# Tracing each group's heads of a state-space mixer ahead of the next group's input products

## The chip, the cores and the metric

The kernel runs on one core of one Trainium2 chip. The metric is the device time of one execution in microseconds (us); lower is better. The engines are named as in the profile: PE (TensorE matmul), PEld (its weight loads), DVE (VectorE), ACT (ScalarE), POOL and SP (which issues the DMAs).

## The reference, cut to what matters

The reference runs a block of two layers and then a second block of two layers on 256 tokens of width 1024. The first block's first layer is an attention mixer and a feed-forward part. Its second layer is the state-space mixer that the change is in (`mamba2_mixer`), followed by a mixture of experts. The second block has two more layers and is not touched.

```python
def mamba2_mixer(h, w_in, conv_w, conv_b, dt_bias, a_log, d_skip, norm_g, w_out):
    proj = h @ w_in
    z = proj[..., :D_INNER]
    xbc = jax.nn.silu(causal_depthwise_conv(proj[..., D_INNER:D_INNER + CONV_DIM], conv_w, conv_b))
    ...
    y = ssd_chunked(xs, dt, a, bm, cm) + d_skip.astype(jnp.float32)[:, None] * xs
    yg = (y * jax.nn.silu(z)).reshape(bsz, seq, SSM_GROUPS, D_INNER // SSM_GROUPS)
    yf = yf * lax.rsqrt(jnp.mean(yf * yf, axis=-1, keepdims=True) + EPS)
    y = (yf.reshape(bsz, seq, D_INNER) * norm_g.astype(jnp.float32)).astype(h.dtype)
    return y @ w_out
```

There are 32 heads of 64 columns in 4 groups of 8. A group thus has 512 columns of `xs` (convolved) and 512 of the gate `z`. A norm is taken over each group by itself, and the output product sums over all four groups (16 slices of 128 rows of `w_out`).

## The kernel before, in words

Activations lie transposed: 128 features on the partitions, 256 tokens along the row. A product takes its weights as float32, loads them by SP in pieces of 1 MB (`load`, tile `raw`, 5 buffers), and splits each piece into two parts of 1024 elements a row: a rounded part `whi` (ACT, L156, 5 buffers) and the rest `wlo` (DVE, L159, 4 buffers). Each 128 x 128 slice of weights then takes three matmuls (`mm3`, L183 to L185). A product of 256 columns over 1024 rows is 48 matmuls into one PSUM bank: `acc` (2 banks) or `s` (3 banks).

The mixer `mamba` first makes `bc` and `dt`, then for each group g four input products in the order conv, z, conv, z. A `conv` product is scaled by ACT (L936), summed over its shifted copies by DVE (L939, three instructions for each 128 columns) and passed through Silu by ACT (L940). A z product is only passed through Silu into `zz[g]` (L1021). For the last group, z is not made there: it is traced behind the heads of group 0, copied (L1080) and passed through Silu later (L1082).

`tokens(g)` transposes a group's `xs` and scales it by `dt` into `xd` (L1032 on PE, L1033 on DVE). `heads(g)` does for each head three small bf16 matmuls into an `s` bank `pe` (L1044 to L1046, here called a triple), three Exp on ACT into `de` (L1049, 2 buffers) and a product with `cb` on DVE into `m` (L1051, 4 buffers). Two heads are then multiplied with `xd` side by side into half of the one `po` bank (L320, eight matmuls, here called a pair), and DVE adds the result into `xs` (L1058). `norm(g)` multiplies `xs` by `zz` (L1061), squares (L256), folds and sums (L239, L241, L249), takes the root (L231, L274 to L278), spreads it (L286, L287) and writes the group's output rows as two parts (L301, L303, L304). These go into slots of a pool of 12 that also holds `xs`, `zz` and the mixer's input `h`.

The output product is 256 columns at a time: `outs[n]` is a generator over the 16 slices of `w_out`, and `next(o)` traces one slice of weights with six matmuls. In the kernel before, the sums for n = 0 and 1 begin in the two `acc` banks at group 0's norm, the one for n = 2 in an `s` bank at the end, and n = 3 after these. `flush` and `route_shift` finish the leftover sums of the modulation vectors (L503, L505) and a router shift (L1107, L1109).

The context is opened with `schedule_with_timeline_sim=True` (L1714). The order in which the instructions are traced is their precedence; a planner makes from it one fixed order for each engine ahead of the run. Where nothing traced earlier is ready by the planner's own times, an instruction that is traced later takes the place. Each engine then works its list strictly in that order.

Of the kernel before, what the change touches and what calls it, by code (L numbers as in the profile page):

```python
# [13 lines left out]
AF = mybir.ActivationFunctionType  # L14
# [6 lines left out]
KT = 8  # L21
# [61 lines left out]
class K:  # L83
# [833 lines left out]
    def mamba(self):  # L917
        nc, i = self.nc, self.i
        v = nc.vector
        w = i["ssm_w_in"][0]  # L920
        self.nslot = 12
        with ExitStack() as c:
            p = c.enter_context(self.tc.tile_pool(name="ssm", bufs=1))
            h = self.xnorm(self.hilo_s(p, KT), self.gs[1][:, 0], self.mod(1, 0), 0)
# [4 lines left out]
            def conv(n0, out):  # L929

                a = self.gemm(w, KT, D * 2 + n0, 256, h, s=n0 == 2560)
                k0 = n0 // P
                for j in range(2):
                    k = k0 + j
                    o = out[:, j]
                    nc.scalar.activation(o, a[:, j], AF.Identity, bias=cb[:, k : k + 1], scale=cw[:, 72 + k : 73 + k])  # L936
                    for s in (1, 2, 3):
                        wc = cw[:, (3 - s) * 24 + k : (3 - s) * 24 + k + 1]
                        v.scalar_tensor_tensor(o[:, s:], a[:, j, : T - s], wc, o[:, s:], ALU.mult, ALU.add)  # L939
                nc.scalar.activation(out, out, AF.Silu)  # L940
# [70 lines left out]
                nc.scalar.copy(t, pc)  # L1011
                cbt.append(t)
            xs, zz = [], []
            for g in range(4):
                xs.append(self.slot(p))
                zz.append(self.slot(p))
                for j in range(2):
                    s2 = slice(2 * j, 2 * j + 2)
                    conv(g * 512 + j * 256, xs[g][:, s2])
                    if g < 3:  # L1020
                        nc.scalar.activation(zz[g][:, s2], self.gemm(w, KT, g * 512 + j * 256, 256, h), AF.Silu)  # L1021
            y = ([], [])
            wo = i["ssm_w_out"][0]
            acc, outs = [], []

            def tokens(g):

                xd = p.tile([P, 2, 8, 64], F32, tag="xd", bufs=2, name=self.name("xd"))
                for t in range(2):
                    px = self.sm([P, 4, P])  # L1030
                    for j in range(4):
                        nc.tensor.transpose(px[:, j], xs[g][:, j, t * P : (t + 1) * P], self.ident)  # L1032
                    v.tensor_mul(xd[:, t], px.rearrange("p j (b e) -> p (j b) e", e=64),  # L1033
                                 dt[:, t, g * 8 : g * 8 + 8].unsqueeze(2).broadcast_to([P, 8, 64]))
                return xd

            def heads(g, xd):
                for j in range(4):
                    if j % 2 == 0:
                        py = self.po()  # L1040
                    for b in range(2):
                        hd = g * 8 + 2 * j + b
                        pe = self.s([P, 3, P])
                        mm(pe, sel[:, hd : hd + 1].broadcast_to([96, P]), r3, start=True, stop=False, skip_group_check=True)  # L1044
                        mm(pe[:, 0], idb, msl, start=False, stop=True, skip_group_check=True)
                        mm(pe[:, 2], idb, msl, start=False, stop=True, skip_group_check=True)  # L1046
                        de = p.tile([P, 3, P], F32, tag="de", bufs=2, name=self.name("de"))
                        for q3 in range(3):
                            nc.scalar.activation(de[:, q3], pe[:, q3], AF.Exp, bias=rb[:, q3, hd : hd + 1])  # L1049
                        m = p.tile([P, 3 * P], F32, tag="m", bufs=4, name=self.name("m"))  # L1050
                        v.tensor_mul(m, de.rearrange("p a b -> p (a b)"), cbt[g])  # L1051
                        o = py[b * 64 : b * 64 + 64, j % 2]
                        if b == 0:
                            av = []
                        av.append([(o, xd[:, 0, 2 * j + b], m[:, :T], True, False), (o[:, P:], xd[:, 1, 2 * j + b], m[:, T:], False, True)])
                    self.side_by_side(*av)
                    o = xs[g][:, j]
                    v.scalar_tensor_tensor(o, o, self.dcol[:, g * 4 + j : g * 4 + j + 1], py[:, j % 2], ALU.mult, ALU.add)  # L1058

            def norm(g):  # L1060
                v.tensor_mul(xs[g], xs[g], zz[g])  # L1061
                t = [self.slot(p, F32R) for _ in range(2)]
                yl = [[s[:, k] for k in range(4)] for s in t]
                for b in range(2):
                    y[b].extend(yl[b])
                self.norm([xs[g][:, j] for j in range(4)], 512, self.cols["ssm_norm"][:, g * 4 : g * 4 + 4], *yl,
                          src=[xs[g][:, j : j + 2] for j in (0, 2)])

            xd = tokens(0)
            for g in range(5):  # L1070
                if g == 1:
                    self.flush()
                    self.route_shift()
                nxt = tokens(g + 1) if g < 3 else None
                if g < 4:
                    heads(g, xd)
                xd = nxt
                if g == 0:
                    for j in range(2):
                        nc.scalar.copy(zz[3][:, 2 * j : 2 * j + 2], self.gemm(w, KT, 1536 + j * 256, 256, h))  # L1080
                if g == 3:
                    nc.scalar.activation(zz[3], zz[3], AF.Silu)  # L1082
                if g:
                    if g == 1:
                        acc = [self.acc() for _ in range(2)]
                        outs = [self.gemm_steps(wo, 16, n * 256, 256, y, acc[n]) for n in range(2)]
                    norm(g - 1)
                    if g == 4:

                        acc.append(self.s())  # L1090
                        outs.append(self.gemm_steps(wo, 16, 512, 256, y, acc[2]))
                        for k in range(12):
                            next(outs[2])
                    for o in outs:
                        for k in range(4):
                            next(o)
            self.hf = self.raw().rearrange("p (k t) -> p k t", k=KT)
            for n in range(4):
                self.resid(acc[n] if n < 3 else self.gemm(wo, 16, 768, 256, y), n * 256, self.mod(1, 2))
# [618 lines left out]
```

## Time and profile before

| | us |
|---|---|
| median of 3 runs | 2644.95 (2644.51 to 2650.42) |
| the profiled execution | 2647.27 |
| its span, first to last instruction | 2645.5 |
| PE busy in the span | 2573.8 (97%) |
| DVE busy | 1972.3 (75%) |
| ACT busy | 1560.9 (59%) |

The span is what lies between the first and the last instruction of the profiled execution. Busy time of PE is pipelined time: an instruction's row is longer than its distance to the next one. A granted clock of 1.00 is 2.4 GHz, and half of it 1.2 GHz. The mixer's loop over groups lies at about 430 to 625 us of the span.

### The profile page before, as it was taken

To read this page: it belongs to the slowest core of one execution; us is meant where nothing else is said; L and a number is where in the kernel's file an instruction comes from. 1 tells how busy PE (TensorE), PEld (TensorE's weight loads), DVE (VectorE), ACT (ScalarE), POOL (GpSimd) and SP (SyncE) were. 2 spreads that over 40 slices of the span, in tenths; PEclk is the share of its full clock that TensorE was granted. 3 is DMA by queue.
4 is the path that set the end of the run, shared out by engine and by line. 5 is a ranking of instruction groups with operands and counts; after the bars stand their busy time and mean duration, and the time that the engine had idled before them with its cause. 6 is when DMAs were issued, how large, how long until landed. Compare 5 with 4: busy or idle time off the path is not lost.

```text
span 2645.5 us, 46204 instructions
## 1 busy us (share of the span) xinstructions
PE 2573.8 (97%) x18463; PEld 2358.8 (89%) x18463; DVE 1972.3 (75%) x3010; ACT 1560.9 (59%) x2189; POOL 6.4 (0%) x27
## 2 busy tenths in 40 slices
PE   8989998989999998999999999999999999999998
PEld 5779998978888887888878999989999999989998
DVE  5776668786999997989888765677665656677664
ACT  4444436674878876777777444675444444675443
POOL 0000000000000000000000000000000000000000
PEclk8989999998999999999999999999999999999999
DMA  9768767416999997999997556525556557525552
GB/s 309 241 230 273 263 188 228 157 60 227 351 363 348 359 372 277 349 363 341 343 368 265 159 176 213 161 69 167 185 175 199 179 180 219 159 65 176 177 182 88
DMA packets 450829, 608.60 MB, mean 230 GB/s; under 512 B 21563, under 2 KB 308816, under 8 KB 450608
## 3 DMA queue, kind: packets, MB, share of 16 engines
q1 hardware_dynamic: 450246, 605.26, 68.4%
q8 instruction: 146, 2.39, 0.4%
q0 software_dynamic: 176, 0.26, 0.1%
q14 instruction: 75, 0.61, 0.1%
q10 hardware_dynamic: 186, 0.07, 0.0%
HBM read 604.50 MB, written 1.05 MB: 229 GB/s over the span
## 4 chain that ended last, share of the span: by engine, by line
PE 59%; DVE 1%; issue 0%; ACT 0%; DVEq 0%; ACTq 0%
PE acc L184 10%; PE acc L183 10%; PE acc L185 10%; PE s L185 3%; PE s L184 3%; PE s L183 3%; PE acc L1283 3%; PE acc L1282 3%; PE acc L1284 3%; PE acc L1306 1%; PE acc L1305 1%; PE acc L1307 1%; PE s L320 1%; PE po L320 1%; PE sm L910 1%; DVE wlo L159 1%
## 5 line engine op out<-in xcount | busy, mean ns | idle before, releaser
L156 ACT CAST whi<-raw 128x1024 fp32r<-128x1024 f32 x816 | 838.6, 1038 | 714.1 <-PE acc L184 431.4
L159 DVE TENSOR_TENSOR wlo<-raw,whi 128x1024 fp32r<-128x1024 f32 x816 | 972.6, 1204 | 292.1 <-PE acc L185 206.0
L183 PE MATMUL acc<-hl,whi 128*128 128x256 f32 x2336 | 668.1, 286 | 6.1 <-DVE s L643 4.6
L184 PE MATMUL acc<-hl,whi 128*128 128x256 f32 x2336 | 663.5, 284 | 1.1 <-DVE hl L308 0.8
L185 PE MATMUL acc<-hl,wlo 128*128 128x256 f32 x2336 | 662.4, 284 | 0.0
L183 PEld LDWEIGHTS acc<-hl,whi 128*128 128x128 f32 x2336 | 443.9, 190 | 9.2 <-DVE s L643 4.8
L184 PEld LDWEIGHTS acc<-hl,whi 128*128 128x128 f32 x2336 | 443.4, 190 | 4.0 <-issue 1.5
L185 PEld LDWEIGHTS acc<-hl,wlo 128*128 128x128 f32 x2336 | 443.4, 190 | 0.6
L159 DVE TENSOR_TENSOR wlo<-more,whi 128x1024 fp32r<-128x1024 f32 x237 | 281.7, 1220 | 20.1 <-PE acc L1283 6.8
L1283 PE MATMUL acc<-wlo,xh 128*128 128x512 f32 (+1 forms) x768 | 288.4, 376 | 0.8
L1282 PE MATMUL acc<-whi,xh 128*128 128x512 f32 (+1 forms) x768 | 288.9, 378 | 0.0
L1284 PE MATMUL acc<-whi,xl 128*128 128x512 f32 (+1 forms) x768 | 285.9, 373 | 0.0
L156 ACT CAST whi<-more 128x1024 fp32r<-128x1024 f32 x237 | 243.1, 1049 | 42.7 <-PE acc L1284 27.0
L184 PE MATMUL s<-hl,whi 128*128 128x256 f32 x880 | 249.1, 283 | 0.0
L185 PE MATMUL s<-hl,wlo 128*128 128x256 f32 x880 | 249.1, 283 | 0.0
L183 PE MATMUL s<-hl,whi 128*128 128x256 f32 x880 | 248.6, 283 | 0.0
L1283 PEld LDWEIGHTS acc<-wlo,xh 128*128 128x128 f32 x768 | 144.4, 188 | 27.9 <-DVE wlo L159 4.4
L1282 PEld LDWEIGHTS acc<-whi,xh 128*128 128x128 f32 x768 | 144.3, 188 | 25.8
L183 PEld LDWEIGHTS s<-hl,whi 128*128 128x128 f32 x880 | 166.8, 190 | 0.0
L1284 PEld LDWEIGHTS acc<-whi,xl 128*128 128x128 f32 x768 | 144.3, 188 | 25.2
L185 PEld LDWEIGHTS s<-hl,wlo 128*128 128x128 f32 x880 | 166.6, 189 | 0.0
L184 PEld LDWEIGHTS s<-hl,whi 128*128 128x128 f32 x880 | 166.5, 189 | 0.0
(477 smaller groups left out, 4065.3 us busy)
## 6 DMA issues: line engine op xcount, KB each, us to landing
raw<-in_moe_w_gate_dram SPq DMA_DIRECT2D x50, 1024.0 KB, 7.3
raw<-in_moe_w_up_dram SPq DMA_DIRECT2D x48, 1024.0 KB, 7.3
raw<-in_ffn_wg_dram SPq DMA_DIRECT2D x44, 1024.0 KB, 5.3
raw<-in_ffn_wu_dram SPq DMA_DIRECT2D x44, 1024.0 KB, 5.3
raw<-in_moe_w_down_dram SPq DMA_DIRECT2D x43, 1024.0 KB, 6.9
more<-in_moe_w_up_dram SPq DMA_DIRECT2D x40, 1024.0 KB, 7.4
more<-in_moe_w_gate_dram SPq DMA_DIRECT2D x38, 1024.0 KB, 6.8
raw<-in_w_in_dram SPq DMA_DIRECT2D x38, 1024.0 KB, 5.4
```

Source lines behind the costliest of these rows:

```text
L156: i = nc.scalar.copy(hi, src[:, k0 : k0 + m])
L159: nc.vector.tensor_sub(lo, src[:, k0 : k0 + m], hi)
L183: mm(out, whi, xhi, start=first, stop=False, skip_group_check=True)
L184: mm(out, whi, xlo, start=False, stop=False, skip_group_check=True)
L185: mm(out, wlo, xhi, start=False, stop=last, skip_group_check=True)
L320: m = self.nc.tensor.matmul(o, w, x, start=start, stop=stop, skip_group_check=True)
L910: nc.tensor.transpose(ptp[:, b * P : (b + 1) * P], pe[:, b * P : (b + 1) * P], self.ident)
L1282: mm(a, xh[:, k], hi, start=k == 0, stop=False, skip_group_check=True)
L1283: mm(a, xh[:, k], lo, start=False, stop=False, skip_group_check=True)
L1284: mm(a, xl[:, k], hi, start=False, stop=k == 7, skip_group_check=True)
L1305: mm(a, fh[k], hi, start=k == 0, stop=False, skip_group_check=True)
L1306: mm(a, fh[k], lo, start=False, stop=False, skip_group_check=True)
```

## The change

The input products of a group become a function `group(g)`, and z of the last group is made like the others (Silu straight from PSUM; the copy and the late Silu are gone). The trace order becomes: group 0; then for g = 0, 1, 2 the heads of g followed by the input products of g + 1; then the tokens of group 3, `flush`, `route_shift`, the norm of group 0, the heads of group 3. Only behind all of these are the three sums of the output opened (n = 0 and 1 in `acc`, n = 2 in an `s` bank), and every step then traces four slices in all three. The norm of group 1 is traced ahead of the first step, the norms of groups 2 and 3 ahead of the second.

```diff
-            for g in range(4):
+            def group(g):
                 ...
                     conv(g * 512 + j * 256, xs[g][:, s2])
-                    if g < 3:
-                        nc.scalar.activation(zz[g][:, s2], self.gemm(w, KT, g * 512 + j * 256, 256, h), AF.Silu)
+                    nc.scalar.activation(zz[g][:, s2], self.gemm(w, KT, g * 512 + j * 256, 256, h), AF.Silu)
...
-            xd = tokens(0)
-            for g in range(5):
+            group(0)
+            for g in range(3):
+                heads(g, tokens(g))
+                group(g + 1)
+            xd = tokens(3)
+            self.flush()
+            self.route_shift()
+            norm(0)
+            heads(3, xd)
+            acc = [self.acc() for _ in range(2)] + [self.s()]
+            outs = [self.gemm_steps(wo, 16, n * 256, 256, y, acc[n]) for n in range(3)]
+            for g in range(4):
+                if g < 2:
+                    norm(g + 1)
                 if g == 1:
-                    self.flush()
-                    self.route_shift()
-                nxt = tokens(g + 1) if g < 3 else None
-                if g < 4:
-                    heads(g, xd)
-                xd = nxt
-                if g == 0:
-                    for j in range(2):
-                        nc.scalar.copy(zz[3][:, 2 * j : 2 * j + 2], self.gemm(w, KT, 1536 + j * 256, 256, h))
-                if g == 3:
-                    nc.scalar.activation(zz[3], zz[3], AF.Silu)
-                if g:
-                    if g == 1:
-                        acc = [self.acc() for _ in range(2)]
-                        outs = [self.gemm_steps(wo, 16, n * 256, 256, y, acc[n]) for n in range(2)]
-                    norm(g - 1)
-                    if g == 4:
-
-                        acc.append(self.s())
-                        outs.append(self.gemm_steps(wo, 16, 512, 256, y, acc[2]))
-                        for k in range(12):
-                            next(outs[2])
-                    for o in outs:
-                        for k in range(4):
-                            next(o)
+                    norm(3)
+                for o in outs:
+                    for k in range(4):
+                        next(o)
```

## Rows read from the trace of the kernel before

**Rows 1.** The page's first part: busy time, share of the span, instructions.

```profile
PE 2573.8 (97%) x18463; PEld 2358.8 (89%) x18463; DVE 1972.3 (75%) x3010; ACT 1560.9 (59%) x2189; POOL 6.4 (0%) x27
```

**Rows 2.** Stretches: length, busy PE, PEld, DVE, ACT, POOL; PE clock, DMA share, GB/s.

```profile
430.00:542.10 112.10, 110.43 (x925) 106.62 (x924) 82.09 (x124) 80.77 (x123) 0.00 (x0) 0.98 0.53 170
542.10:609.00 66.90, 58.50 (x469) 50.48 (x468) 53.96 (x138) 40.61 (x97) 0.00 (x0) 0.95 0.19 64
...
440.00:460.00 20.00, 18.33 (x158) 17.39 (x158) 17.06 (x25) 17.70 (x31) 0.00 (x0) 1.00 0.68 228
...
563.00:575.00 12.00, 8.29 (x73) 5.12 (x69) 11.85 (x38) 9.15 (x32) 0.00 (x0) 1.00 0.27 87
```

**Rows 3.** Groups of PE instructions from 542.1 to 609 us.

```profile
L183 PE MATMUL acc<-g,whi 128*128 128x256 f32 x65 | 18.5, 295 | 1.4 <-ACT g L303 1.4
L183 PE MATMUL s<-g,whi 128*128 128x256 f32 x32 | 9.1, 285 | 0.5 <-ACT whi L156 0.5
L320 PE MATMUL po<-m,xd 128*64 128x256 f32 x44 | 7.6, 427 | 2.0 <-DVE m L1051 1.3 <-DVE g L1058 0.7
L1044 PE MATMUL s<-r,sel 96*128 96x384 bf16 x18 | 5.7, 332 | 1.4 <-ACT de L1049 1.1
L287 PE MATMUL sm<-dg,ones 128*128 128x128 f32 x16 | 3.5, 325 | 2.8 <-DVE dg L286 2.7
L1032 PE MATMUL sm<-cst,g 128*128 128x128 f32 x8 | 1.7, 345 | 0.0
L249 PE MATMUL sm<-ones,sq 128*128 128x1 f32 x12 | 1.6, 234 | 0.0
```

**Rows 4.** PE in order of time: the pace of undisturbed matmuls, first and last of 47.

```profile
592.37 0.28 PE L183 MATMUL s<-g,whi 128*128 128x256 f32 x1
...
597.82 0.28 PE L184 MATMUL s<-g,whi 128*128 128x256 f32 x1
```

**Rows 5.** PE in order of time, around the end of the input products and after.

```profile
542.33 0.87 PE L320 MATMUL po<-m,xd 128*64 128x256 f32 x8
543.13 0.34 PE L1044 MATMUL s<-r,sel 96*128 96x384 bf16 x1
...
543.42 0.33 PE L1044 MATMUL s<-r,sel 96*128 96x384 bf16 x1
...
546.80 0.69 PE L287 MATMUL sm<-dg,ones 128*128 128x128 f32 x2 [2.67 <-DVE dg L286]
...
584.16 0.54 PE L183 MATMUL acc<-g,whi 128*128 128x256 f32 x2 [0.99 <-ACT g L303]
...
585.51 0.41 PE L183 MATMUL acc<-g,whi 128*128 128x256 f32 x1
```

**Rows 6.** Groups of DVE instructions from 542.1 to 609 us.

```profile
L1051 DVE TENSOR_TENSOR m<-de,cb 128x384 f32<-128x384 f32 x19 | 10.4, 552 | 3.4 <-ACT de L1049 3.1
L1058 DVE SCALAR_TENSOR_TENSOR g<-g,dcol,po 128x256 f32<-128x256 f32 x11 | 5.2, 473 | 0.0
L606 DVE SCALAR_TENSOR_TENSOR xT<-acc,mod,xT 128x256 f32<-128x256 f32 x4 | 1.8, 480 | 6.1 <-PE acc L185 6.1
L159 DVE TENSOR_TENSOR wlo<-raw,whi 128x1024 fp32r<-128x1024 f32 x10 | 12.1, 1222 | 3.1 <-PE acc L185 2.5 <-PE s L185 0.6
```

**Rows 7.** PE and then ACT in order of time, heads between two z products.

```profile
457.46 0.22 PE L1046 MATMUL s<-msl,idb 128*128 128x128 bf16 x1
459.33 0.39 PE L183 MATMUL acc<-g,whi 128*128 128x256 f32 x1 [1.65 <-ACT g L1021]
...
453.73 1.66 ACT L1049 ACTIVATE de<-s,rb 128x128 f32<-128x128 f32 x6
455.24 2.13 ACT L156 CAST whi<-raw 128x1024 fp32r<-128x1024 f32 x2
457.38 1.28 ACT L1021 ACT_TABLE_LOAD   x1
458.68 0.60 ACT L1021 ACTIVATE g<-acc 128x512 f32<-128x512 f32 x1
```

## The prediction, as it was put on record

> **What bounds the kernel now.** I read the page's first part, then the busy time by stretch of the mixer, then PE in order of time there, and last the groups of DVE and ACT instructions. PE is busy for 97% of the span [rows 1], so time can only come from places where PE waits, and the stretches show them. From 430 to 542.1 us, while input products are left, PE is busy 110.43 of 112.1 us. From 542.1, the end of the last z product, to 609.0, the end of the three interleaved output sums, it is busy 58.50 of 66.9 us, with the granted clock at 0.95 on the mean [rows 2]. I call them the input stretch and the tail. From 609 to 625 us the fourth output product runs alone and I expect nothing of it to change.
>
> Busy PE is not PE at its peak, so I price the tail's work. Forty-seven undisturbed matmuls span 5.45 us, 0.1185 us each [rows 4]. The tail has 97 slices of three [rows 3]: 291 x 0.1185 = 34.5 us. It has eleven pairs (44 of the wide L320 form, four to a pair) at 0.80 us, the distance to the next instruction [rows 3, 5]: 8.8 us. Its 18 triples [rows 3] lie 0.29 us apart [rows 5]: 5.2 us. The 36 transposes, sums and spreads [rows 3], taken at the plain pace of 0.12 us, are 4.3 us. Together 52.8 us, so 14.1 of the 66.9 us are lost. The largest single loss is at 543.9 us, where PE waits 2.67 us for the norm's spread. Matmuls after the wait at 584 us are 0.21 us apart instead of 0.12: that is 1.2 GHz in place of 2.4 [rows 5]. In the middle of the tail DVE is the one that is full: 11.85 of 12 us from 563 to 575, with PE at 8.29 [rows 2]. So the tail is held by the elementwise work of 18 late heads and of the norms, for which there are too few products to run beside.
>
> **The change part by part.**
>
> *Work moved out of the tail.* Behind the last z product only the four pairs of group 3 need be left, and I take six triples (two heads done ahead; `m` has room for four, so four to eight). Seven pairs (5.6 us), twelve triples (3.5) and the four transposes of the last tokens (0.5) go: 9.6 us of PE work moves into the input stretch. That stretch has 1.67 us of idle PE, so all 9.6 us lengthen it. No matmul is saved.
>
> *The tail that is left.* PE: 52.8 - 9.6 = 43.2 us. DVE: 53.96 us [rows 2] less twelve `m` at 0.55 (6.6), seven L1058 at 0.47 (3.3), and the 1.8 us of L606 that follow the sums [rows 6]: 42.3 us. ACT had 40.61 us [rows 2] and loses twelve heads of Exp (36 at 0.28 us, by six in 1.66 [rows 7]) and the copy and Silu of the last z, so it does not govern. PE and DVE are nearly even, therefore neither hides the other's start and end. I add 5 us: the wait for the first output rows (here 1.4 us by L303 [rows 3]), the wait at the last norm (0.99 in the row, some 2 with the gaps beside it) and one stretch at the lower clock [rows 5]. The bounds are 0 (everything beside products) and 14.1 (as lost before). Tail after: 48.2 us, 18.7 less.
>
> *Three output sums instead of two from the first step.* This is what gives PE products while the norms of groups 1 to 3 and heads 3 run: 72 matmuls (8.5 us) a step instead of 48. Each stream holds the second half of its split weights until the next group's rows are there. With four `wlo` buffers and three streams one buffer is free, and a split takes some 2.3 us (DVE 1.22 in [rows 6], ACT some 1.05 in [rows 7]) against 2.8 us for the 24 matmuls of a chunk. It fits without a margin; if DVE is late, up to six splits of 2.3 us would show (13.8), if not, nothing. I put it inside the 5 us. The third `s` bank is asked for behind the last heads, so these have three banks first. The same eight loads of 1 MB go through SP, in another order, with the DMA engines 19% busy in the tail [rows 2]; at nothing.
>
> *Heads ahead of the next input products.* Now their instructions go first wherever they are ready, on PE, ACT and DVE. What waits behind them is the next group's splits, convolution and Silu, and through the two `acc` banks PE. By totals there is room: PE 112.1 + 9.6 us, DVE 82.09 + 9.9, ACT 80.77 and 10 for twelve heads of Exp at 0.28 each [rows 2, 7]. The order is the question. One such place exists: at 457.5 us, with the heads of group 0 just run, PE waits for a z product to leave its bank, because ACT does casts, loads the table for Silu (1.28 us) and only then empties it; the distance is 1.87 us, 1.8 of it lost [rows 7]. I take one such stall for each of the three head groups inside the input stretch: 5.4 us, against 1.67 us there before: +3.7. The bounds: none at all (-1.7), and one for each of the four Silus a group, twelve in all (21.6, +19.9).
>
> *The last z with the others, `flush` and `route_shift` ahead of norm 0.* The copy of the last z and its late Silu were ACT work with a table load on either side; its removal is in the tail's numbers. The one-column sums and the router shift are the same matmuls in another place, at nothing; the low clock behind them (some 1.7 us) may come elsewhere, so -1.7 to +1.7.
>
> **Sum:** -18.7 (tail) + 9.6 (work moved) + 3.7 (stalls) = -5.4 us. The profiled execution took 2647.27 us, its span 2645.5 and 1.77 us lie around it; with the change 2641.9. The median before is 2.32 us below that execution, so for a median I expect 2644.95 - 5.4 = 2639.5.
>
> What the Trainium skill would make of it stands by itself. The page "ScalarE: Activation LUTs", section "Rules for kernel authors", says to group functions by table set and finish one set before switching, and its section "What ACT_TABLE_LOAD costs" gives about 2.66 us a switch with the drain. The change mixes Exp with Silu, so the rule speaks against it. This case's rows show 1.28 us for the load and the next instruction right behind it [rows 7]. By the page's price each stall would be 1.4 us dearer and the sum about -1.2 us.
>
> **The rivals.**
>
> *B, no new stall.* The planner finds places for the heads, and DVE and PE overlap all but 2 us of the tail: -21.7 + 9.6 = -12.1, 2632.9. For it: in the input stretch PE waits only 1.67 us although 14 heads already run there, and from 460 us on there is no wait to speak of. Against: those heads filled gaps; now they come first.
>
> *C, the tail stays held by DVE.* The four norms and the last heads are a chain through DVE, and DVE was full where PE waited. Group 3 has its own heads, then its norm, and the norms of groups 2 and 3 both come ahead of the second step. If 10 us of the 14.1 remain lost, the tail is 53.2 (-13.7) and the sum -13.7 + 9.6 + 3.7 = -0.4: 2644.5. The planner doing by itself most of what the new order asks for ends here too, as the first heads already run among the products of group 1.
>
> *D, slower: ACT's tables stop PE in the input stretch.* Each group has four Silus. If Exp of the heads lies between each two of them, ACT switches eight times a group (10.2 us by the load's 1.28), each bank is emptied late, and each time PE loses 1.8 us as at 457.5 [rows 7]: -18.7 + 9.6 + 19.9 = +10.8, 2655.8. It turns the result from six stalls on (6 x 1.8 - 1.67 = 9.1, the rest of the sum). For it: where heads came close together, from 440 to 460 us, ACT was busy 17.70 of 20 us and PE lost 1.67. Against: `acc` has two banks and a product takes 5.7 us, so one late Silu alone does not reach PE; and eight heads in a row need one load.
>
> **How the numbers follow.** My forecast (A, 2636 to 2643 by itself) gets 0.40, B 0.25, C 0.22, D 0.13. The range leaves out the best of B and most of D: 2630 to 2650. A measurement of this kernel tells about 0.3%, 7.9 us, from no change, so faster means below 2637.0 and slower above 2652.9. Faster: B and a quarter of A, 0.35. Slower: most of D, 0.10. Same: 0.55.
>
> **What would show it.** The last L1058 should lie close behind the last input product, with four or five of them after it instead of eleven; that product should end near 555 us instead of 542.1 and the third output sum near 603.5 instead of 609. PE from 563 to 575 should no longer stand at 8.29 of 12. The prediction is wrong if PE waits for the emptying of `acc` more than six times in the input stretch (D), if DVE is full after its end while PE idles 10 us (C), or if the last input product ends before 553 us with no waits (B).

## The result and the profile after

With the change the kernel takes 2666.64 us (median of 4 runs, 2665.5 to 2668.08); the kernel before, run beside it, took 2647.68. The ratio is 1.007, 95% interval 1.0057 to 1.0083: slower by 0.7%, where 2639.5 was forecast. The profiled execution took 2666.73 us, its span 2664.9.

The first part of the page after, to be compared with [rows 1]: the same 18463 matmuls, 7 us more busy time of PE, five more ACT instructions.

```profile
PE 2581.2 (97%) x18463; PEld 2364.0 (89%) x18463; DVE 1973.8 (74%) x3010; ACT 1571.6 (59%) x2194; POOL 6.5 (0%) x27
```

The mixer can be measured by itself from two events that every kernel here has: the last copy of the B/C products ahead of the change (L1011 on ACT, the second row of its pair) and the last L606 on DVE, which is the residual of the fourth output product. Before, in order of time:

```profile
437.53 0.48 ACT L1011 COPY cb<-s 128x384 f32<-128x384 f32 x1 [0.18 <-PE s L1009]
624.90 0.88 DVE L606 SCALAR_TENSOR_TENSOR xT<-acc,mod,xT 128x256 f32<-128x256 f32 x2 [8.99 <-PE acc L185]
```

After:

```profile
440.22 0.48 ACT L1011 COPY cb<-s 128x384 f32<-128x384 f32 x1 [0.18 <-PE s L1009]
648.56 0.88 DVE L606 SCALAR_TENSOR_TENSOR xT<-acc,mod,xT 128x256 f32<-128x256 f32 x2 [9.62 <-PE acc L185]
```

That is 187.4 us before and 208.3 after: the mixer is 20.9 us longer. In every run here 3170 matmuls start ahead of the first event, yet it comes 2.7 us later after; and from the last L606 to the end of the span it is 2016.3 us instead of 2020.6. Two later kernels whose mixer is untouched gave 188.0 (that of before) and 207.2 (that of after), so this "mixer length" repeats to about 1 us in these two pairs. It is what I compare below, beside the medians.

Stretches of after. The first two end where the last input product ends (562.5) and where the output products begin in earnest (591); they are to be compared with [rows 2].

```profile
430.00:562.50 132.50, 122.86 (x1008) 112.65 (x1008) 93.53 (x144) 100.97 (x170) 0.00 (x0) 0.99 0.45 143
562.50:591.00 28.50, 21.36 (x109) 16.54 (x108) 16.26 (x48) 12.37 (x27) 0.00 (x0) 0.59 0.11 37
591.00:636.00 45.00, 41.98 (x333) 41.16 (x332) 33.09 (x86) 18.99 (x32) 0.00 (x0) 0.96 0.29 94
570.00:580.00 10.00, 9.46 (x45) 8.11 (x45) 0.93 (x4) 1.13 (x3) 0.00 (x0) 0.50 0.01 2
580.00:590.00 10.00, 7.89 (x36) 5.16 (x37) 8.60 (x33) 4.11 (x11) 0.00 (x0) 0.50 0.00 0
```

The second stretch is the new thing: 28.5 us with 109 matmuls, at a mean clock of 0.59, and neither DVE nor ACT full. From 570 to 590 the clock is 0.50, that is 1.2 GHz, while PE counts as busy for 9.46 of the first 10 us: a busy share alone would not have shown it. The DMA engines stand nearly still (0.01 and 0.00), so no load of weights is under way that PE could be waiting for. PE in order of time through it:

```profile
562.27 0.28 PE L185 MATMUL acc<-g,wlo 128*128 128x256 f32 x1
...
566.78 0.66 PE L1034 MATMUL sm<-cst,g 128*128 128x128 f32 x4 [2.96 <-ACT g L940]
569.47 3.52 PE L503 MATMUL sm<-ones,ada 128*128 128x1 f32 x16
574.47 3.53 PE L1101 MATMUL sm<-wr,mod 128*128 128x8 f32 x16
577.85 0.99 PE L249 MATMUL sm<-ones,sq 128*128 128x1 f32 x4
580.64 1.55 PE L320 MATMUL po<-m,xd 128*64 128x256 f32 x8 [1.18 <-DVE g L1060]
588.69 0.80 PE L183 MATMUL acc<-g,whi 128*128 128x256 f32 x2
```

The order is that of the tracing: tokens of group 3 (L1034), `flush` (L503), `route_shift` (L1101), sums of norm 0 (L249), and the first output product (L183 into `acc`) 26 us behind the last input product. DVE beside it has its two long idle times just there, 8.35 us together, both ended by the small matmuls:

```profile
573.02 0.17 DVE L505 TENSOR_TENSOR mod<-sm,colsa 128x8 f32<-128x8 f32 x1 [3.50 <-PE sm L503]
578.04 0.17 DVE L1103 COPY sw<-sm 128x8 f32<-128x8 f32 x1 [4.85 <-PE sm L1101]
```

PE's waits from 420 to 660 us (total, times, longest). The first row is the emptying of `acc` by the Silu of z. All of it lies ahead of 562.5, and its five waits stay below the "more than six" that the prediction named as the mark of rival D:

```profile
PE acc L183 <- ACT g L1022: 7.4, 5, 2.4
...
PE sm L1034 <- ACT g L940: 3.3, 2, 3.0
PE s L1046 <- ACT de L1051: 2.8, 2, 1.5
PE po L320 <- DVE g L1060: 2.6, 3, 1.2
```

Table loads on ACT from 430 to 650 us, after: 23 up to the mixer's end, 29.5 us. (The kernel before has 17 in the same places, 21.8 us.)

```profile
L1051 ACT ACT_TABLE_LOAD x12 | 15.4, 1283 | 0.2
L1022 ACT ACT_TABLE_LOAD x6 | 7.7, 1283 | 0.1
L940 ACT ACT_TABLE_LOAD x5 | 6.4, 1283 | 1.0 <-DVE g L939 0.9
```

### The profile page after: what moved, and what is told of

Same layout as the page of the kernel before. It is cut to its first block, busy times and chain, and to the rows that moved or that the text cites. A ratio compares the mean times of both kernels' runs of the same rounds, so it can differ in the third digit from the quotient of the medians.

```text
span 2664.9 us, 46216 instructions
## 1 busy us (share of the span) xinstructions
PE 2581.2 (97%) x18463; PEld 2364.0 (89%) x18463; DVE 1973.8 (74%) x3010; ACT 1571.6 (59%) x2194; POOL 6.5 (0%) x27
## 4 chain that ended last, share of the span: by engine, by line
PE 58%; DVE 1%; issue 0%; ACT 0%; DVEq 0%; ACTq 0%
PE acc L184 10%; PE acc L183 10%; PE acc L185 9%; PE s L185 3%; PE s L184 3%; PE s L183 3%; PE acc L1277 3%; PE acc L1276 3%; PE acc L1278 3%; PE acc L1300 1%; PE acc L1299 1%; PE acc L1301 1%; PE s L320 1%; PE po L320 1%; PE sm L910 1%; DVE wlo L159 1%
## 5 line engine op out<-in xcount | busy, mean ns | idle before, releaser
L183 PE MATMUL acc<-hl,whi 128*128 128x256 f32 x2336 | 667.8, 286 | 6.2 <-DVE s L643 4.6
L183 PEld LDWEIGHTS acc<-hl,whi 128*128 128x128 f32 x2336 | 443.4, 190 | 9.3 <-DVE s L643 4.8
L183 PE MATMUL s<-hl,whi 128*128 128x256 f32 x880 | 248.7, 283 | 0.0
L183 PEld LDWEIGHTS s<-hl,whi 128*128 128x128 f32 x880 | 166.5, 189 | 0.0
```

The lines of the kernel that those rows point to most:

```text
L183: mm(out, whi, xhi, start=first, stop=False, skip_group_check=True)
```

## The experiments

All were timed in three or five rounds beside the kernel before; a median is of 4 to 11 runs. "Mixer" is the length defined above, from each kernel's one profile.

| kernel | median us | ratio, 95% | mixer us |
|---|---|---|---|
| after | 2666.64 | 1.0070 (1.0057 to 1.0083) | 208.3 |
| e1_flush_early | 2664.44 | 1.0057 (1.0040 to 1.0073) | 207.6 |
| e2_norm0_ahead | 2664.90 | 1.0056 (1.0036 to 1.0075) | 202.9 |
| e3_after_one_table | 2654.57 | 1.0024 (1.0013 to 1.0035) | 193.4 |
| e4_before_one_table | 2643.68 | 0.9980 (0.9969 to 0.9990) | 183.3 |
| e5_norms_ahead | 2667.12 | 1.0075 (1.0055 to 1.0095) | 207.0 |
| e6_norms_ahead_one_table | 2655.23 | 1.0025 (1.0016 to 1.0034) | 195.1 |
| e7_groups_first | 2653.96 | 1.0018 (1.0008 to 1.0027) | 191.6 |
| e8_before_gathered | 2647.88 | 0.9992 (0.9983 to 1.0001) | 186.9 |
| e9_two_norms_ahead | 2653.41 | 1.0025 (1.0014 to 1.0036) | 199.5 |
| e10_three_sums_only | 2651.80 | 1.0017 (1.0006 to 1.0028) | 192.4 |
| e11_lagged_heads | 2647.77 | 1.0000 (0.9990 to 1.0010) | 197.2 |
| e12_lagged_gathered | 2655.66 | 1.0031 (1.0020 to 1.0042) | 194.7 |
| e13_lagged_two_sums | 2657.95 | 1.0032 (1.0021 to 1.0044) | 197.3 |
| e14_after_two_sums | 2669.35 | 1.0081 (1.0066 to 1.0096) | 203.6 |
| e15_norms_two_sums | 2665.22 | 1.0065 (1.0052 to 1.0078) | 204.3 |
| e16_groups_first_norms | 2648.02 | 0.9999 (0.9990 to 1.0008) | 188.6 |
| e18_before_update_behind | 2645.52 | 0.9990 (0.9981 to 0.9999) | 188.0 |
| e19_after_update_behind | 2666.63 | 1.0074 (1.0061 to 1.0088) | 207.2 |

**The small matmuls and the norms of the tail.** e1_flush_early: `flush` and `route_shift` behind the first heads.

```diff
 for g in range(3):
+    if g == 1: self.flush(); self.route_shift()
     heads(g, tokens(g))
     group(g + 1)
 xd = tokens(3)
-self.flush(); self.route_shift()
```

> The changed kernel with flush and route_shift traced before the heads of group 1 and not behind the tokens of group 3. Theory T (two causes of about equal size: in the input stretch the table loads between Exp and Silu stop PE; in the tail the tokens of group 3, the leftover sums, the router shift and the first norm's sums share the two sm banks in the order of the tracing, so nothing of norm 0 comes before the last input product, and PE runs 32 narrow matmuls at 1.2 GHz meanwhile): the 32 narrow matmuls leave the tail, 7 us at half clock there against 3.4 us in the input stretch, and norm 0 comes some 5 us earlier: 6 to 12 us below the changed kernel, 2655 to 2661. Rival R (the tail is held by the chain of the last heads and norms through DVE, whatever stands between): within 3 us of the changed kernel's 2666.6.

The router shift, 3.53 us in after, is shorter among input products:

```profile
497.58 1.85 PE L1102 MATMUL sm<-wr,mod 128*128 128x8 f32 x16
```

But the mixer is only 0.7 us shorter, and the median within 3 us of after, as the rival had it. The time was lost elsewhere: from the last matmul of the input products to the first output product it is 19.5 us (568.13 to 587.67) instead of 26.4, but that last matmul stands 5.6 us further behind the mixer's first event than in after:

```profile
568.13 0.28 PE L185 MATMUL acc<-g,wlo 128*128 128x256 f32 x1
```

e2_norm0_ahead: norm 0 ahead of tokens 3.

```diff
+norm(0)
 xd = tokens(3)
 self.flush(); self.route_shift()
-norm(0)
```

> The changed kernel with the norm of group 0 traced ahead of the tokens of group 3, flush and route_shift staying behind these. Theory T: the first norm's sums then have an sm bank before the last input product, the first output rows are there soon after it, and output products run beside the leftover sums and the last heads: 8 to 15 us below the changed kernel, 2652 to 2659; the sums of norm 0 (L249) stand before the last input product. Rival R: within 3 us of 2666.6.

Norm 0's rows came 15 us earlier (572.65), the mixer was 5.4 us shorter; norm 1's were not earlier by as much (595.27 instead of 598.11), since tokens 3 and the flush now stood ahead of it. The median fell by 1.7 us only, which misses the theory's 2652 to 2659: in the place 850 us further on that is described below, e2 takes 4.3 us longer than after (853.6 against 849.3).

e5_norms_ahead: flush early as in e1, and

```diff
-xd = tokens(3); flush; route_shift; norm(0); heads(3, xd)
+for g in range(3):
+    norm(g)
+heads(3, tokens(3))
```

> The changed kernel with flush and route_shift ahead of the heads of group 1 and the norms of groups 0, 1 and 2 traced ahead of the tokens of group 3. Theory T' (after the first two runs: what holds the tail is that every norm's sums and spread take an sm bank in the order of the tracing; moving flush alone or norm 0 alone leaves norm 1 and 2 behind tokens 3, some 10 us each one after the other): the sums (L249) of norms 0 to 2 then stand before or at the end of the input products, the tail shrinks from 69 us to 50 to 57, and the kernel takes 2648 to 2656. Rival R' (norms and last heads are DVE work that only moves into an input stretch that is already held by ACT and DVE): 2661 to 2668, as in the two runs before.

No gain: with three norms ahead, the heads of group 3 ended at 610 and norm 3's rows came at 619. The theory fell, and the time is the rival's: what is put first makes the other late.

e9_two_norms_ahead: flush early, norms 0 and 1 ahead of tokens 3, norm 2 behind heads 3.

> The changed kernel with flush and route_shift ahead of the heads of group 1, the norms of groups 0 and 1 ahead of the tokens of group 3, and norm 2 behind the heads of group 3. Theory U (the tail is a chain of norms, each some 10 to 12 us from its sums to its rows, after tokens 3 and heads 3; with three norms ahead the tokens of group 3 were the late ones, xd at 595 us): now neither is late, heads 3 end before 590 and the third sum near 615 to 620: 2650 to 2658. Rival V (the input stretch pays for what the tail gains, whatever the place): 2662 to 2668.

The median fell by 13.2 us, the mixer by 8.8; the rest of the gain is not the mixer's (below). The time is thus in the theory's range in part by luck, and the heads of group 3 ended at 600, not before 590. The first output product started at 573.63 instead of 588.69. The mixer has 27 table loads here, four more than after, and is still shorter: the number of loads does not order these times.

**The tables.** e3_after_one_table and e4_before_one_table: Identity for the Silu of the groups' x and z, in the kernel after and before. Both compute another function by it and serve for the time alone.

```diff
-conv(..., xs[g][:, s2])                       # Silu
-nc.scalar.activation(zz[g][:, s2], ..., AF.Silu)
+conv(..., xs[g][:, s2], AF.Identity)
+nc.scalar.activation(zz[g][:, s2], ..., AF.Identity)
```

> The changed kernel with Identity in place of Silu for the convolutions and z of the four groups (so another function is computed there), which takes the table loads between Exp and Silu away and leaves PE's and DVE's lists as they are. Theory T: of the some 11 us that the input stretch loses on PE more than before, the waits behind L1022, L940 and de go: 8 to 13 us below the changed kernel, 2654 to 2659. Rival Q (the stretch loses its time to the order alone: heads first delay casts and convolutions): less than 3 us.

> The kernel before with the same replacement (Identity for Silu in the four groups). Theory T: it has fewer loads in places that stop PE (457.5 us, 539 to 550 us), so it gains 3 to 6 us, less than the changed kernel does from the same edit: 2639 to 2642. Rival Q: within 2 us of 2645.

Only one table load of the mixer is left in each. The edit takes out little else: e3 has the DVE and ACT instructions of after in the same order, and the matmuls too but for one swap at 2398 us, far behind the mixer; Identity takes as long as Silu (L1022 0.59 us against 0.60, L940 0.64 against 0.63). After became 12 us faster, its mixer 14.9 shorter; before 4 us faster, its mixer 4.1 shorter (against the kernel before of its own rounds, 2648.22, it gains 4.5 us, within the 3 to 6 expected, though its time is above 2642). So some 10.8 of the 20.9 us go by what table loads cost more in the new order than in the old one. PE's waits of e3 from 436 to 570 us show where:

```profile
PE po L320 <- DVE g L1060: 2.6, 3, 1.2
PE acc L183 <- ACT g L1022: 2.6, 4, 1.6
PE sm L1034 <- ACT g L940: 0.8, 1, 0.8
```

Against after, the waits for the emptying of `acc` fall from 7.4 to 2.6 us, those for the tokens from 3.3 to 0.8, and the last input product ends at 551.8. The two kernels with one table still differ by 10.1 us, so the tables are about half of it.

e6_norms_ahead_one_table is e5 with Identity.

> The same with Identity for Silu in the four groups (another function is computed there), so without the table loads. If the two causes, table loads and norms behind tokens 3, are separate, their gains add: 10 to 14 us below the run with the norms ahead, 2636 to 2644, which is below the kernel before. If they are the same waits seen twice: no more than 5 us below that run, or no lower than 2650.

11.9 us less than e5, as separate causes would have it, but far above the 2636 to 2644 named for them, and no better than e3: that order gains nothing without the loads either.

e8_before_gathered: in the kernel before, x and z leave PSUM by plain copies, and one Silu for x and one for the group before's z follow.

```diff
-conv(...); nc.scalar.activation(zz[g][:, s2], gemm, AF.Silu)   # twice a group
+conv(..., False); nc.scalar.copy(zz[g][:, s2], gemm)
+last = nc.scalar.activation(xs[g], xs[g], AF.Silu)
+# zz[g - 1] right behind last
```

> The kernel before with the two Silus of a group's convolutions gathered into one over 1024 columns and the z of a group copied first and passed through Silu right behind the next group's convolutions; it computes the same. If table loads cost the kernel before what the run with one table showed (4.5 us), ten loads fewer give most of that back: 2640 to 2644 against a kernel before at 2645 to 2648. If the loads it saves hide beside products: within 2 us of before.

Eight loads fewer (9 of 17 are left), and no measurable gain. The heads ended 1.3 us later behind the mixer's first event, and PE waited once 3.7 us for an Exp, which stood behind the Silu of the last z and its loads; why the loads saved give nothing back is not shown further.

**Heads ahead of the input products.** e7_groups_first: all else as in after.

```diff
-group(0)
-for g in range(3):
-    heads(g, tokens(g))
-    group(g + 1)
+for g in range(4): group(g)
+for g in range(3): heads(g, tokens(g))
```

> The changed kernel with the four groups' input products traced first, as before, and the heads of groups 0 to 2 behind them; the last z with the others, flush, norms, heads 3 and the three sums stay as changed. Theory T': the waits of the input stretch mostly go (8 to 11 us), but 18 heads are back in the tail beside three sums that start behind all heads, so the tail is longer than the 66.9 us of before: 2655 to 2670. Rival (the trace order of the heads alone made the loss): back to 2644 to 2650.

12.7 us of the median and 16.7 of the mixer come back, and the table loads of the mixer are 17 again, as before. This one part of the change costs most of it. The time, 2653.96, lies between the two expectations. The 4.2 us by which this mixer is still longer than before's are near the 5.0 that the three sums alone cost there (e10, below).

e11_lagged_heads: e9 with each heads(g) behind group(g + 1).

> As the run with two norms ahead, but the heads of a group are traced behind the input products of the next group instead of ahead of them (one group later). Theory W (precedence is what costs in the input stretch: heads that come first put Exp and table loads before the emptying of acc): the waits behind z (L1022, 4 to 7 us) fall under 3 us and the kernel takes 2645 to 2653, at least 5 us below that run. Rival (the stretch is full whatever the order): within 3 us of it.

Level with the kernel before by its median, but its mixer is 9.8 us longer. Against e9 the waits for `acc` behind z fall from 4.3 to 2.8 us, as expected, and the median by 5.6 us, but the mixer only by 2.3.

e12_lagged_gathered: e11 with the gathered Silu of e8.

> The same with the two Silus of a group's convolutions gathered into one and z copied first and passed through Silu right behind the next group's convolutions (same result). Eight or more table loads fewer should give 3 to 8 us, to 2640 to 2647, which may be below the kernel before; if the waits are of the order alone, within 2 us of the run without.

The median says 8 us worse, the mixer 2.5 us better. The place below makes 6.8 us of the difference.

e16_groups_first_norms: groups first as in e7, norms as in e9.

> The four groups' input products traced first, then the heads of groups 0 to 2 with flush and route_shift behind the first, norms 0 and 1 ahead of the last tokens, three sums behind. Read at the mixer's last L606 (before 624.9, changed kernel 648.6, groups first with the changed tail 634.1, norms in time with heads ahead 637.8). If order of heads and order of norms add: 622 to 626. Rival: with the heads late the norms can't be early, and it ends at 630 to 635.

Its mixer is 1.2 us longer than before's: neither answer was met (the last L606, at 628.6, lies between the two), and a new trace order of the same parts finds the old time again, no more. Heads traced ahead cost 16.7 us with the change's tail (208.3 to 191.6) and 10.9 with norms in time (199.5 to 188.6).

**The three sums.** e10_three_sums_only: in the kernel before.

```diff
-acc = [self.acc() for _ in range(2)]        # third opened in the last step
+acc = [self.acc() for _ in range(2)] + [self.s()]
```

> The kernel before with all three sums of the output opened at group 0's norm and stepped together, nothing else changed. If three streams on four wlo buffers cost what the run with the groups first lost (4.9 us more than before): 2649 to 2653. If that loss is from the place of flush and the norms: 2642 to 2648, at best faster by the products that fill the waits at 563 to 575 us.

The mixer is 5.0 us longer. PE's first wait from 540 to 610 us of it; in the kernel before that row is one wait of 2.67 [rows 5]:

```profile
PE sm L287 <- DVE dg L286: 5.6, 2, 3.0
```

e13_lagged_two_sums, e14_after_two_sums and e15_norms_two_sums open the third sum ahead of the last step instead, in e11, after and e9.

> The lagged-heads order (2647.77, level with the kernel before) with two output sums first and the third opened ahead of the last step. If the third sum costs by holding split buffers and moving DVE's splits ahead of the norms in any order: 4.5 us come back as on the kernel before, 2643 (2641 to 2645), norm 2's rows some 5 to 8 us earlier. Rival: the price on the kernel before was of its order alone (late heads and splits on DVE); here heads are done earlier, PE has gaps that the third sum fills, and taking it out leaves 2648 to 2652.

> The changed kernel with two output sums first and the third opened ahead of the last step. Theory that the third sum costs 4.5 us by itself: 2662 (2660 to 2664). Rival: in the changed kernel the chain of norms, 10 to 12 us each, sets the tail, and the third sum only fills the gaps of PE beside it; without it 48 matmuls of some 0.12 us (5.8 us) fall behind the last norm: 2666 to 2672.

> The order with flush early and norms 0 and 1 ahead of the last tokens (2653.41), with two output sums first. If the terms add: 2649 (2647 to 2651), which would leave some 4 us to the mixing of heads and input products. Rival: no gain once the norms come in time, 2653 to 2656.

The mixer moved by 0.1, -4.7 and +4.8 us, the medians by +10.2, +2.7 and +11.8. Of the median's rise 8.2 us in e13 and 5.0 in e15 come with the place below; both medians lie above either expectation. The third sum has no one price: between these orders even its sign changes. On after itself it is open: by the mixer e14 agrees with the theory, by its median with the rival.

**A wait 850 us further on.** e9 and e11 gained more in all than in the mixer. From the last L606 to the first gate multiply of the last SwiGLU (L643) the kernel before takes 852.0 us, e9 844.3 and e11 844.5; the others with that place unedited lie between 849.0 and 853.6. PE's waits of the kernel before, from 1420 to 1540 us:

```profile
PE acc L183 <- DVE s L643: 4.6, 1, 4.6
```

The row stands in all but e9 and e11. DVE in order of time, in the kernel before:

```profile
1473.41 0.42 DVE L592 COPY rb<-sm 128x256 f32<-128x256 f32 x1
1473.75 3.21 DVE L597 SCALAR_TENSOR_TENSOR xT<-xT,colsb,sm 128x256 f32<-128x256 f32 x8
1476.88 0.68 DVE L643 TENSOR_TENSOR s<-acc,rb 128x512 f32<-128x512 f32 x1
```

and in e11:

```profile
1479.40 0.42 DVE L592 COPY rb<-sm 128x256 f32<-128x256 f32 x1 [0.58 <-PE sm L287]
1479.85 0.48 DVE L597 SCALAR_TENSOR_TENSOR xT<-xT,colsb,sm 128x256 f32<-128x256 f32 x1
1480.25 1.28 DVE L643 TENSOR_TENSOR s<-acc,rb 128x512 f32<-128x512 f32 x2
```

Eight updates of the residual stand ahead of the first gate in the one, one in the other. Thirty us around that place, first in the kernel before, then in e11 (clock 0.86 and 1.00):

```profile
1460.00:1490.00 30.00, 25.44 (x190) 25.25 (x190) 23.80 (x52) 11.83 (x14) 0.00 (x0) 0.86 0.40 123
```

```profile
1464.00:1494.00 30.00, 30.00 (x256) 30.00 (x256) 26.27 (x59) 14.28 (x16) 0.00 (x0) 1.00 0.56 175
```

66 matmuls fewer at 0.1185 us [rows 4] are 7.8 us, about the whole of the 7.5 by which e11 is shorter from the mixer to here. e18_before_update_behind and e19_after_update_behind hold the eight updates until the second gate has left PSUM.

```diff
-    nc.vector.tensor_mul(s, a, rb)
+    gate = nc.vector.tensor_mul(s, a, rb)
 ...
-    update()
+    with self.tc.issue_after(gate.ins):
+        update()
```

> The kernel before, with the eight multiplies that update xT in the last SwiGLU (L597, 3.21 us on DVE) held until its second pair of gates is out of PSUM, so that the first gate multiply (L643) no longer waits for them. The mixer is left alone: its last L606 stays at 624.9. If the one wait of 4.6 us and the lower clock beside it come from these eight: 3 to 9 us less, 2638 to 2645. Rival: the first gate waits for the norm itself, and the eight only fill DVE's time until then: within 1 us of the kernel before.

> The changed kernel with the same eight multiplies held. As on the kernel before: 3 to 9 us less than 2666.64, 2658 to 2664, with the mixer's last L606 at 648.6 as in the changed kernel. If the place is worth the same in both, the comparison of before and after is not touched by it, and the gain of the two kernels without the wait was by that much not the mixer's.

The wait is left in both, in e18 so:

```profile
PE acc L183 <- DVE s L644: 2.1, 1, 2.1
```

2.5 us of the 4.6 are gone. e18's median is 2.6 us under the kernel before (ratio 0.999, interval 0.9981 to 0.9999), the expectation missed at its edge; e19's median is that of after and misses its expectation; 2.6 us less could not be seen beside the spread of its runs (2661.6 to 2669.72). By the profiles the way to L643 is 3 us shorter in each (848.9 instead of 852.0, 846.4 instead of 849.3), but e8 and e16 had 849.0 without the edit. So the updates account for 2.5 us of the wait and not for the 7.5 of the place; what else is earlier in e9 and e11 stays open. For before against after it does not matter, as both have the wait.

e18 is the fastest that computes the same function, though hardly: no order of the mixer tried here beats the old one.

## Why the prediction was wrong

**The sum.** Forecast was -5.4; the mixer alone gave +20.9. By its terms, from the last L1011:

*Work moved and stalls, +9.6 and +3.7.* The last input product should have ended 117.9 us behind the mark (555.4 - 437.53) and ended 122.3 behind it (562.5 - 440.22): 4.4 us over. The work moved is as forecast: four L1058 are left behind the product. The mis-sized term is the stalls. I counted one stall for each group of heads, 5.4 us of idle PE in all; there were five waits for `acc`, 7.4 us, and with smaller waits PE is idle for 132.50 - 122.86 = 9.6 us from 430 to 562.5. Without the loads the product ends at 551.8 - 438.82 = 113.0, 9.3 us earlier. Rival D had the cause (the tables), but of its twelve stalls, 21.6 us, only five came, 7.4 us; and it had the place too narrow: by its count of waits it looks refuted, by e3 the tables are half the loss. In this kernel a late ACT shows as waits for `acc`, for tokens, for Exp, and in the tail, where 2.96 of the 3.3 us for tokens lie.

*The tail that is left, 48.2 us.* This is the step that failed most. From 562.5 to the end of the third sum, about 631.4 (its L606 at 631.67), it is 68.9 us: 20.7 over.

```profile
631.67 0.87 DVE L606 SCALAR_TENSOR_TENSOR xT<-s,mod,xT 128x256 f32<-128x256 f32 x2
```

I summed PE's work and DVE's work and put "5 us for start and end" on them. But with heads 3 and all the norms left, what ends the tail is a chain, not a sum: tokens 3 wait for a Silu, 32 small matmuls stand next on PE, then norm 0, and its rows (588) come 26 us after the last input product, with a PE that has no input or output products to run and stands at 1.2 GHz from 568 on. The bound of 14.1 that I gave, "as lost before", was no bound: in the kernel before the first output product ran 10 us behind the last input product, and here 26 us:

```profile
552.26 0.50 PE L183 MATMUL acc<-g,whi 128*128 128x256 f32 x2
```

From the last input matmul to the L606 of the third sum it is 69.4 us in after, 63.6 in e3 without the loads and 57.2 in e9 with `flush` early and the norms in time (564.29 to 621.54). e9 pays some 4 us of that in the input stretch and keeps 8.8 of the mixer; e1, e2 and e5 show that no single edit of the chain does as much. Why even e9's tail is some 8.5 us above the forecast 48.2 stays open.

*The three sums "inside the 5 us".* Opened from the first step they cost 5.0 us of the mixer in the kernel before, save 4.8 in e9's order, and cost 4.7 of the mixer in the kernel after, though not of its median: no sum by PE's and DVE's totals could have given that.

*`flush` and `route_shift` "at nothing".* In their new place they hold PE from 569.47 to 577.85 while DVE waits 8.35 us, outside my +-1.7. That they gave only 0.7 back when moved (e1) is because the input stretch became 5.6 us longer by it, while the way to the first output product behind it became 6.9 shorter.

*The fourth product, "nothing to change".* From third to last L606 15.6 us before, 16.9 after: +1.3. With the two terms above, 4.4 + 20.7 + 1.3 = 26.4, and -5.4 + 26.4 = 21.0.

**The rivals.** C's mark, a full DVE while PE idles, is not there: DVE is 16.26 of 28.5 us busy. What the forecast lacked was a stretch in which no engine is full. Tables (some 10.8 us, e3 against e4) and order of norms (8.8, e9) make 19.6 of the 20.9; heads ahead (16.7, e7) and three sums (5.0, e10) make 21.7. Both sums come near, and their terms overlap: e7 brings the loads back to 17, and norms in time are worth 3.0 with the groups first (e7 and e16). So each cause is shown, and the split is not.

**The page's rule.** The Trainium skill, "ScalarE: Activation LUTs", section "Rules for kernel authors", has functions grouped by table set. That speaks against the change, and e3 agrees: 12.1 us of the median. The number of loads did not decide: each took 1.28 us, e9 has four more than after and is faster, and gathering the Silus (e8, e12) saved loads while PE waited longer for Exp (3.7 us once in e8, 5.1 once in e12).

## What to carry to other kernels

Price what is left behind the last big product as a chain, instruction by instruction in trace order with the engine that runs each, and only then compare it with the sums of PE and DVE; the independent products that ran beside it in the old order were its cover. An order change moves the planner's choices far behind it too: compare the changed stretch between two fixed events, not only the total, or a wait 850 us later is put down to the edit, as the medians of e11, e12 and e13 would have it. Here the table loads cost by what they delayed, not by their own time (22 of them 14.9 us in the one order, 16 of them 4.1 in the other), so take them all out at once before saying what they are worth.

## What the runs showed of the hardware

Small float32 matmuls kept PE counted as busy at half clock: sixteen of eight columns took 3.53 us at 574.47 (0.22 us each, granted clock 0.50), and 1.85 us in e1, among input products (0.12 us each, granted clock 1.00); that is about what a matmul of 256 columns takes there (0.1185 [rows 4]). From 570 to 580 us the busy share alone, 9.46 of 10, would call PE full; the clock column and the 0.93 us of DVE and 1.13 of ACT show how little ran beside it. The clock fell before the small matmuls and not by them: it is 0.93 on the mean from 564 to 568 us, where PE is busy for 0.66 of 4 us, and 0.50 from 568 to 570, while the first small matmul starts at 569.47. From 591 on, with output products, it is 0.96 on the mean.

```profile
564.00:568.00 4.00, 0.66 (x4) 0.49 (x5) 3.13 (x6) 3.95 (x5) 0.00 (x0) 0.93 0.46 160
568.00:570.00 2.00, 1.02 (x6) 0.85 (x5) 1.11 (x2) 1.99 (x9) 0.00 (x0) 0.50 0.00 0
```
